# Key tiles of 8 grid rows by 16 columns in a neighbourhood attention, in place of 16 by 8

## The chip, the cores and the metric

The kernel runs on one core of a Trainium2 chip. The metric is the device time of one execution in microseconds. Before the change the median of three runs is 632.16 us (632.13 to 632.43).

## The reference

One layer over 1024 latent tokens on a grid of 16 rows by 64 columns and 256 context tokens, width 1024. A conditioned RMS norm and one input projection give eight groups of 512 columns; half feed an attention of 8 heads of 64, half a gated short convolution; both are gated, joined and projected out. Cut to the attention:

```python
row_start = clip(qi - 4, 0, rows - 8)            # 8 rows of keys for each query row
col_start = clip(cols - 8, 0, 64 - 16)           # 16 columns of keys for each query column
s_lat = (q_rot . k_rot) * scale + rpb[dr, dc]    # -inf outside the window
s_ctx = (q_plain . kc) * scale                   # all 256 context keys
p = softmax(concat(s_lat, s_ctx))
o = p_lat @ v + p_ctx @ vc
```

All of it is in float32, and the kernel keeps that precision by splitting each operand into a high and a low part and multiplying three times (`mm3`, line 68), or twice in the scores, where the two halves of a query lie below each other in the 128 partitions.

## The kernel before

**Order of tokens.** After the norm, the transposed activations are stored block by block: 8 blocks of 128 tokens, a block being 16 grid rows by 8 columns (`rows_of`, line 686; `blocked`, `by_row`, `natural`, lines 378 to 385). Block j is therefore also key tile j. Everything after the projection sees tokens in this order until the output projection puts them back (`put_y`).

**Projection.** 32 tiles (four pairs of heads by eight token blocks) are projected in the loop at the end of the projection stage; `turn_qk` (line 237) transposes queries and keys of two blocks, splits them in high and low and spills them to DRAM. In the same loop `bias_tables` (line 749) spreads the padded bias in DRAM by two rounds of transfers on SyncE's queue (SP), and `masked_tables` (line 928) adds the window mask and stores one table of 128 by 3 by 384 for each head.

**Attention.** The loop at line 1360 calls `quarter(n)` (line 1110) for n = 0 to 35; n is a *tick*, four to a head, called quarters g = n % 4 here. The order of instructions on every engine is fixed by the order in which the code emits them (`strict`, line 1355). In tick n, TensorE does

- the maxima of quarter e = n - 2: `pmx` transposes two blocks of the running maximum `mx`, VectorE reduces them (`rm`), `pmx` spreads them back and ScalarE copies them to `mg`;
- the context products of quarter o = n - 3 (`ctx_out`), in `po`;
- the scores of two key tiles of tick n (`scores`, in `pss`): tile j against the query blocks j-1 to j+1, which is 384 columns, or 256 at the edges. A head's tiles go 0; 1, 2; 3, 4; 5, 6; 7, and tile 7 shares a tick with tile 0 of the next head, so that 33 ticks have scores;
- the context scores of quarter n (`ctx_scores`, in `pc`);
- steps of *filler*: the rest of the projection (`pu`, six matmuls of 512 columns a step); `TICKS[n]` (line 33) says how many;
- between them the value products of tick o (`lat_out`, `pv`, lines 1048 to 1058), three per tile and PSUM bank, added up in two banks of 512 query columns for each head. Tiles 3 and 4 straddle the border of the banks.

In the same tick VectorE adds the bias to the scores, updates `mx` with the context (`ctx_max`) and the two tiles (`lat_max`), subtracts the maximum from those of quarter e, makes the low parts of the exponentials (`plc`, `pll`), and does what the filler needs (`ul`, `cv`). ScalarE takes each exponential twice, once rounded and once whole. At the end of a bank `finish` copies it out and stores it. Loads for the next head are issued from SP during the head before (lines 1360 to 1368).

Of the kernel before, what the change touches and what calls it, by code (L numbers as in the profile page):

```python
# [19 lines left out]
P = 128  # L20
D = 1024
T = 1024
# [10 lines left out]
TICKS = [2, 3, 3, 3, 3, 2, 3, 3, 2] + 2 * (8 * [3] + 2 * [4]) + 3 * [3] + [4, 4, 3, 2]  # L33
# [6 lines left out]
def body(tc, es, x, ctxt, w_ada, b_ada, w_in, q_g, k_g, rpbr, w_out, vecs, cst, out):  # L40
# [196 lines left out]
    def turn_qk(pp, p, two, t0):  # L237
# [140 lines left out]
    def blocked(v):  # L378
        return v.rearrange("p (b r c) -> p b r c", b=4, r=16)

    def by_row(v):
        return v.rearrange("p (r b c) -> p b r c", r=16, b=4)

    def natural(v, half):
        return v.rearrange("p (r b c) -> p b r c", r=16, b=8)[:, 4 * half:4 * half + 4]

    def blocked8(v):
        return v.rearrange("p (b r c) -> p b r c", b=8, r=8)
# [8 lines left out]
    def conv_group(i, done=None):  # L397
# [10 lines left out]
        def multiplied(half, ps):  # L408
            def product():
                to, of = (rows8(cu[:, 1:T + 1], half, 8), blocked8) if done else (natural(cu[:, 1:T + 1], half), blocked)  # L410
# [47 lines left out]
        def gains():  # L458
            for half, ps in sorted(done[CBG].items()) if done else ():
                for q in range(2):  # L460
                    def gain(half=half, ps=ps, q=q):
                        v = rows8(cvs[q][:], half, 4)
                        dve.tensor_tensor(v, blocked8(ps[:])[:, 4 * q:4 * q + 4], v, ALU.mult)
# [205 lines left out]
    def modulated(hi, lo, ps, k, w, on, between=None):  # L669
# [5 lines left out]
        if n == 512:  # L675
            hv = hv.rearrange("p (r b c) -> p r b c", r=8, b=8)
# [9 lines left out]
    def rows_of(v, half):  # L686

        return v.rearrange("p (b r c) -> p r b c", b=8, r=16)[:, 8 * half:8 * half + 8]
# [7 lines left out]
    def turn(half, k, on, between=None):  # L696

        modulated(rows_of(hh[k], half), rows_of(hl[k], half),
                  pts.pop((half, k))[:].rearrange("p (r b c) -> p r b c", r=8, b=8), k, 0, on, between)
# [49 lines left out]
    def bias_tables():  # L749

        for kc in range(8):
            sp.dma_start(t2_d[kc], bass.AP(rpbr.tensor, rpbr.offset + 7 - kc, [[31, NH * 31], [1, 24]]))
        t2 = t2_d[:]
        for kr in range(16):
            if kr % 4 == 0:
                yield
            sp.dma_start(t3_d[:, kr], bass.AP(t2.tensor, t2.offset + (15 - kr) * 24,
                                              [[744, NH], [NH * 744, 8], [1, 384]]))
# [169 lines left out]
    def masked_tables():  # L928
# [3 lines left out]
        view = lambda t, n: t.rearrange("p (o r c) -> p o r c", r=16, c=8)  # L932
        for h in range(NH):
            raw = bmp.tile([P, 512], F32, name="braw", tag="kc_s", bufs=2)
            sp.dma_start(raw[:, :384], t3_d[h].rearrange("a b c -> (a b) c"))
# [4 lines left out]
            stores.append(lambda h=h: sp.dma_start(t4_d[h], bt[:].rearrange("p v n -> p (v n)")))  # L940
# [43 lines left out]

    class head:
# [27 lines left out]
        def masks(self):  # L1013
            self.bt = bmp.tile([P, 3, 384], F32, name="bt", tag="bt", bufs=2)
            sp.dma_start(self.bt[:].rearrange("p v n -> p (v n)"), t4_d[self.h])

        def ctx_scores(self, g):
# [6 lines left out]
            sc = ap.tile([P, 2, 256], F32, name="sc", tag="sc", bufs=3)  # L1024
# [8 lines left out]
        def span(self, j):  # L1033
            return max(j - 1, 0), min(j + 1, NB - 1)

        def scores(self, j, ps):
            lo, hi = self.span(j)
            n = (hi - lo + 1) * P
            q = self.q[:, 0, lo * P:(hi + 1) * P]
            for l in range(2):  # L1040
                pe.matmul(ps[:, :n], self.k[:, j // 2, l, j % 2 * P:(j % 2 + 1) * P], q, start=(l == 0), stop=(l == 1))

        def lat_max(self, j, sb):
            lo, hi = self.span(j)
            m = mx[:, lo * P:(hi + 1) * P]
            dve.tensor_tensor(m, m, sb[:, :(hi - lo + 1) * P], ALU.max)

        def pv(self, bank, cols, j, ph, pl, last):
# [3 lines left out]
            o_ = self.po[bank][0:HD + 1, cols]  # L1052
# [5 lines left out]
        def lat_out(self, j, ph, pl):  # L1058
            lo, hi = max(j - 1, 0), min(j + 1, NB - 1)
            for a, b in ((lo, min(hi, 3)), (max(lo, 4), hi)):  # L1060
                if a <= b:
                    src = slice((a - lo) * P, (b + 1 - lo) * P)
                    self.pv(a // 4, slice((a % 4) * P, (b % 4 + 1) * P), j,
                            ph[:, src], pl[:, src], (a // 4, j) in ((0, 4), (1, 7)))

        def ctx_exp(self, g):
# [3 lines left out]
            ph = ap.tile([P, 2, 256], F32R, name="phc", tag="phc", bufs=2)  # L1070
            pl = ap.tile([P, 2, 256], F32R, name="plc", tag="plc", bufs=2)
# [5 lines left out]
        def ctx_out(self, g):  # L1077
            ph, pl = self.cps.pop(g)
            for i in range(2):
                self.pv(g // 2, slice((g % 2) * 256, (g % 2 + 1) * 256), NB + i, ph[:, i], pl[:, i], False)  # L1080

        def finish(self, bank):

            ob = ap.tile([P, 512], F32, name="ob", tag="ob", bufs=1)
            act.copy(ob[0:HD + 1], self.po[bank][0:HD + 1])
# [3 lines left out]
    def pair_of(n):  # L1089

        h, g = divmod(n, 4)
        two = [(h, 0), (h - 1, 7)] if g == 0 else [(h, 2 * g - 1), (h, 2 * g)]
        return [(i, heads[h_], j) for i, (h_, j) in enumerate(two) if 0 <= h_ < NH]

    def both(v, n, pair):
# [428 lines left out]
```

## Time and profile before

| | |
|---|---|
| median of three runs | 632.16 us |
| the profiled execution, in all | 632.35 us |
| its span in the trace | 630.6 us |
| TensorE busy | 624.0 us |
| VectorE busy | 439.1 us |
| ScalarE busy | 330.0 us |
| granted TensorE clock | 1.00 |
| first scores of the attention | 267.1 us |
| last filler of the attention ends | 539.3 us |

How to read it: PE is the matmuls of TensorE, PEld its weight loads, DVE is VectorE, ACT is ScalarE, POOL is GpSimd, SP is SyncE. Names such as `po<-phl,v` give the tile written and the tiles read, without buffer numbers. Nearly every instruction of these stages passes through one helper and has line 55, so groups are told apart by their tiles. The chain of waits follows the work that ended last back in time; its rows give a start, a length, and a number of instructions. A row of the busy time by stretches gives the stretch, its length, the busy time and the number of instructions of PE, PEld, DVE, ACT and POOL, the granted clock, the share of DMA and its GB/s.

### The profile page before, as it was taken

What the parts mean: (1) busy time and instruction counts of PE and PEld (TensorE: products, weight loads), DVE (VectorE), ACT (ScalarE), POOL (GpSimd) and SP (SyncE); (2) the same over time, 40 slices, a digit from 0 to 9 for tenths busy, and PEclk for the clock granted to TensorE, in tenths of its full rate; (3) what the DMA queues carried; (4) which work ended last, traced back from release to release, by engine and by line L of the source; (5) the groups of instructions that cost most, each with busy time, mean ns of one, the idle gap of its engine ahead of it and who ended that gap; (6) DMA issues with size and microseconds to landing.
All of it is one profiled execution on the core that took longest, in us unless ns stands there. A gap on an engine that the chain in (4) does not pass through costs nothing.

```text
span 630.6 us, 9908 instructions
## 1 busy us (share of the span) xinstructions
PE 624.0 (99%) x3439; PEld 537.1 (85%) x3440; DVE 439.1 (70%) x874; ACT 330.0 (52%) x713; POOL 77.6 (12%) x102
## 2 busy tenths in 40 slices
PE   8999999999999999999999999999999999999998
PEld 3577899999999999888888888888888888888887
DVE  1887859766857755468888889987998865593211
ACT  4676835425625446346676568567775855460000
POOL 1305014123123222000000000000000002002300
PEclk9999999999999999999999999999999999999999
DMA  8983638867775994965383636683842234962731
GB/s 316 358 286 116 180 110 263 258 196 221 267 244 164 295 328 147 324 228 186 129 289 118 217 90 214 191 273 105 271 126 75 60 99 130 374 222 77 268 101 50
DMA packets 103006, 125.60 MB, mean 199 GB/s; under 512 B 9665, under 2 KB 71577, under 8 KB 101676
## 3 DMA queue, kind: packets, MB, share of 16 engines
q1 hardware_dynamic: 96492, 113.38, 54.4%
q10 hardware_dynamic: 6208, 11.05, 5.5%
q0 software_dynamic: 256, 0.54, 0.3%
q8 instruction: 27, 0.44, 0.3%
q14 instruction: 23, 0.19, 0.1%
HBM read 88.09 MB, written 38.62 MB: 201 GB/s over the span
## 4 chain that ended last, share of the span: by engine, by line
PE 98%; DVE 1%; issue 0%; POOL 0%; ACT 0%; POOLq 0%
PE pu L55 30%; PE pacc L55 21%; PE po L55 8%; PE acc L55 6%; PE tr L55 5%; PE pout L75 5%; PE pout L76 5%; PE pout L74 5%; PE cacc L55 4%; PE pss L55 3%; PE pmx L55 2%; PE pc L55 2%; PE trA L55 1%; PE trB L55 1%; POOL xss L55 0%
## 5 line engine op out<-in xcount | busy, mean ns | idle before, releaser
L55 PE MATMUL pu<-h,uh 128*128 128x512 f32 x544 | 169.4, 392 | 0.6 <-DVE cv L55 0.6
L55 PE MATMUL pacc<-w,h 128*128 128x384 f32 x768 | 138.4, 337 | 0.0
L55 PEld LDWEIGHTS pacc<-w,h 128*128 128x128 f32 x768 | 132.7, 188 | 0.2
L55 PEld LDWEIGHTS pu<-h,uh 128*128 128x128 f32 x544 | 98.1, 188 | 18.2 <-DVE cv L55 1.0
L55 PE MATMUL pu<-h,ul 128*128 128x512 f32 x272 | 106.4, 391 | 0.0
L55 PEld LDWEIGHTS pu<-h,ul 128*128 128x128 f32 x272 | 51.1, 188 | 11.3
L55 POOL TENSOR_TENSOR ss<-ss,few 128x4 f32<-128x4 f32 (+1 forms) x40 | 41.9, 1048 | 124.8 <-DVE ss L55 124.8
L75 PE MATMUL pout<-wol,yh 128*128 128x512 f32 (+2 forms) x136 | 51.6, 379 | 0.0
L74 PE MATMUL pout<-woh,yh 128*128 128x512 f32 (+2 forms) x136 | 50.5, 379 | 0.0
L76 PE MATMUL pout<-woh,yl 128*128 128x512 f32 (+2 forms) x136 | 49.8, 379 | 0.0
L55 PE MATMUL acc<-h,w 128*128 128x512 f32 x144 | 38.1, 404 | 0.8 <-ACT h L55 0.8
L55 ACT ACTIVATE sq<-pacc 128x256 f32<-128x256 f32 x32 | 12.3, 386 | 49.1 <-PE pacc L55 47.5
L55 ACT COPY mg<-pmx 128x256 f32<-128x256 f32 x32 | 11.9, 373 | 43.3 <-PE pmx L55 40.8
L55 DVE TENSOR_REDUCE rm<-pmx 128x2 f32<-128x256 f32 x32 | 13.6, 425 | 30.1 <-PE pmx L55 29.8
L55 DVE TENSOR_TENSOR mx<-mx,sb 128x384 f32<-128x384 f32 (+1 forms) x64 | 33.0, 524 | 2.0
L55 DVE TENSOR_REDUCE ss<-sq 128x4 f32<-128x260 f32 (+1 forms) x40 | 15.7, 392 | 23.9 <-ACT sq L55 23.9
L55 ACT ACTIVATE qn<-pacc,ss 128x64 f32<-128x64 f32 x128 | 30.1, 331 | 3.0 <-issue 2.5
L55 PE MATMUL po<-phl,v 128*65 128x256 f32 (+2 forms) x160 | 31.2, 291 | 0.0
L55 PEld LDWEIGHTS acc<-h,w 128*128 128x128 f32 x144 | 25.5, 188 | 6.5 <-ACT h L55 1.2
L55 ACT COPY sc<-pc 128x512 f32<-128x512 f32 x32 | 18.8, 589 | 22.7 <-PE pc L55 22.6
L55 DVE TENSOR_TENSOR pll<-sb,phl 128x768 fp32r<-128x768 f32 (+2 forms) x33 | 28.4, 861 | 1.9 <-ACT sb L55 1.9
L74 PEld LDWEIGHTS pout<-woh,yh 128*128 128x128 f32 x136 | 25.6, 188 | 4.7
(159 smaller groups left out, 1176.7 us busy)
## 6 DMA issues: line engine op xcount, KB each, us to landing
uraw<-in_w_in SPq DMA_DIRECT2D x34, 256.0 KB
q_d<-qs SPq DMA_DIRECT2D x32, 256.0 KB
k_s<-k_d SPq DMA_DIRECT2D x8, 1024.0 KB
q_s<-q_d SPq DMA_DIRECT2D x16, 512.0 KB
wr<-in_w_in SPq DMA_DIRECT2D x40, 192.0 KB
slab<-in_w_ada SPq DMA_DIRECT2D x6, 1024.0 KB
v_d<-vs SPq DMA_DIRECT2D x20, 260.0 KB
v<-v_d SPq DMA_DIRECT2D x16, 325.0 KB
```

Of the source, the lines that this page charges most:

```text
L55: i = emit(*a, **kw)
L74: i = pe.matmul(ps, ah, bh, start=first, stop=False)
L75: pe.matmul(ps, ah, bl, start=False, stop=False)
L76: pe.matmul(ps, al, bh, start=False, stop=last)
```

## The change

A block of 128 tokens becomes 8 grid rows by 16 columns: tile j holds columns 16 (j // 2) onward and the upper or lower eight rows. Tokens in the blocked activations follow as 4 column blocks by 16 rows by 16 columns. Queries are stored column by column, 16 rows to a column: `turn_qk` reorders them while it splits them. A key tile of the upper rows is seen by query rows 0 to 11 only, one of the lower rows by rows 4 to 15, and by the columns from 7 before its own to 8 after; so a tile is multiplied with 12 of every 16 values of a run of 24, 31, 31 or 23 columns.

With it:

- A tick takes the two tiles of one column block, 32 ticks have scores, and the loop has 35 ticks; the last four numbers of `TICKS` become three with the same sum.
- Value products write 12 of every 16 columns of a bank; the column ranges 9 to 40 and 25 to 56 straddle the border at column 32.
- The bias and mask tables become 2 by 47 by 12 in place of 3 by 384; the bias sum takes two instructions in the first and last quarter of a head, one in the others.
- Blocks of the maximum now end half a quarter later: tick n turns blocks 2e + 1 and 2e + 2, so that tick 1 turns block 0 of the first head, and tick 33 the last block.
- Context scores and maxima run one tick ahead (tick 0 does quarters 0 and 1); their copies get four buffers in place of three, the context exponentials one in place of two.
- `finish` reorders a bank while it copies it. Rotary tables and the padded bias are laid out to match on the host.

```diff
-TICKS = [2, 3, 3, 3, 3, 2, 3, 3, 2] + 2 * (8 * [3] + 2 * [4]) + 3 * [3] + [4, 4, 3, 2]
+TICKS = [2, 3, 3, 3, 3, 2, 3, 3, 2] + 2 * (8 * [3] + 2 * [4]) + 3 * [3] + [4, 5, 4]
...
-    t2_d = dr.tile([8, NH * 31, 24], F32, name="t2_d")
-    t3_d = dr.tile([NH, 16, 8, 384], F32, name="t3_d")
-    t4_d = many("t4_d", NH, [P, 3 * 384])
+    t2_d = dr.tile([8, NH * 47, 16], F32, name="t2_d")
+    t3_d = dr.tile([NH, 8, 16, 512], F32, name="t3_d")
+    t4_d = many("t4_d", NH, [P, 1128])
...
-            halves(qs[:, 0], qs[:, 1], pA[:].rearrange("p k i d -> p k (i d)"))
+            halves(*(qs[:, l].rearrange("p k (c r) -> p k c r", r=16) for l in range(2)),
+                   pA[:].rearrange("p k i d -> p k (i d)").rearrange("p k (r c) -> p k c r", r=16))
...
-        h_, l_ = (v.rearrange("p (b r c) -> p b (r c)", b=8, r=16)[:, :, 64 * half:64 * half + 64]
+        h_, l_ = (v.rearrange("p (b r c) -> p b (r c)", b=4, r=16)[:, :, 128 * half:128 * half + 128]
...
-            for n in range(3):
-                dve.tensor_tensor(view(bt[:, n], n), raw[:, :384].rearrange("p (r o c) -> p o r c", r=16, c=8),
-                                  view(mk[:, n], n), ALU.add)
+            by_col = raw[:].rearrange("p (c r) -> p c r", r=16)
+            for a in range(2):
+                rows = slice(4 - 4 * a, 16 - 4 * a)
+                for to, of in ((slice(0, 31), slice(0, 31)), (slice(31, 47), slice(7, 23))):
+                    dve.tensor_tensor(flat(bt)[:, a, to], by_col[:, of, rows], mk[:, a, to], ALU.add)
...
+    def span(j):
+
+        return max(j // 2 * 16 - 7, 0), min(j // 2 * 16 + 24, GW)
+
+    def seen(v, j, cols=None):
+
+        lo, hi = cols or span(j)
+        return v.rearrange("p (c r) -> p c r", r=16)[:, lo:hi, 4 * (j % 2):4 * (j % 2) + 12]
+
+    def cells(v, j, cols=None):
+
+        at = span(j)
+        lo, hi = cols or at
+        return v[:, (lo - at[0]) * 12:(hi - at[0]) * 12].rearrange("p (c r) -> p c r", r=12)
...
         def scores(self, j, ps):
-            lo, hi = self.span(j)
-            n = (hi - lo + 1) * P
-            q = self.q[:, 0, lo * P:(hi + 1) * P]
+            q = seen(self.q[:, 0], j)
             for l in range(2):
-                pe.matmul(ps[:, :n], self.k[:, j // 2, l, j % 2 * P:(j % 2 + 1) * P], q, start=(l == 0), stop=(l == 1))
+                pe.matmul(cells(ps, j), self.k[:, j // 2, l, j % 2 * P:(j % 2 + 1) * P], q, start=(l == 0), stop=(l == 1))
...
-            for a, b in ((lo, min(hi, 3)), (max(lo, 4), hi)):
-                if a <= b:
-                    src = slice((a - lo) * P, (b + 1 - lo) * P)
-                    self.pv(a // 4, slice((a % 4) * P, (b % 4 + 1) * P), j,
-                            ph[:, src], pl[:, src], (a // 4, j) in ((0, 4), (1, 7)))
+            lo, hi = span(j)
+            for bank in range(2):
+                at = max(lo, 32 * bank), min(hi, 32 * bank + 32)
+                if at[0] < at[1]:
+                    self.pv(bank, lambda o: seen(o, j, (at[0] - 32 * bank, at[1] - 32 * bank)), j,
+                            cells(ph, j, at), cells(pl, j, at), (bank, j) in ((0, 5), (1, 7)))
...
+    def turned(n):
+
+        g = n % 4
+        return [b for b, there in (((2 * g + 2) % NB, n + 1 < 4 * NH), (2 * g + 1, n >= 0)) if there][::-1 if g < 3 else 1]
...
-        if live(e):
-            hd, g = heads[e // 4], e % 4
+        blocks = turned(e) if -1 <= e < 4 * NH else []
+        nb = len(blocks)
+        if blocks:
             pm = psm.tile([P, 512], F32, name="pmx", tag="C", bufs=2)
-            for i in range(2):
-                pe.transpose(pm[:, i * P:(i + 1) * P], mx[:, (2 * g + i) * P:(2 * g + i + 1) * P], ident)
+            for i, b in enumerate(blocks):
+                pe.transpose(pm[:, i * P:(i + 1) * P], mx[:, b * P:(b + 1) * P], ident)
...
-        if live(n):
-            heads[n // 4].ctx_scores(n % 4)
+        ctx_now = [m for m in ([0, 1] if n == 0 else [n + 1]) if live(m)]
+        for m in ctx_now:
+            heads[m // 4].ctx_scores(m % 4)
...
+            for at, slot, w_ in (((0, 31, 8), (8, 15, 16)), ((0, 0, 31),), ((0, 0, 31),), ((0, 0, 15), (15, 39, 8)))[n % 4]:
+                dve.tensor_tensor(sb[:, :, at * 12:(at + w_) * 12], sbank[:, :, at * 12:(at + w_) * 12],
+                                  bt[:, :, slot * 12:(slot + w_) * 12], ALU.add)
+            for m in ctx_now:
+                heads[m // 4].ctx_max(m % 4)
...
-        for n in range(4 * NH + 4):
+        for n in range(len(TICKS)):
```

More of the change, by code (lines that the diff above doesn't have):

```diff
@@ L698, in turn @@
         modulated(rows_of(hh[k], half), rows_of(hl[k], half),
-                  pts.pop((half, k))[:].rearrange("p (r b c) -> p r b c", r=8, b=8), k, 0, on, between)
+                  pts.pop((half, k))[:].rearrange("p (r b c) -> p r b c", r=8, b=4), k, 0, on, between)
     def transposed_ctx(k2):
@@ L1131, in quarter @@
             gating.pop(0)
-        if live(e):
-            for i in range(2):
+        if blocks:
+            for i in range(nb):
                 pe.transpose(pm[:, 256 + i * P:256 + (i + 1) * P], rm[:, i:i + 1].broadcast_to([P, P]), ident)
-            act.copy(mg[:, g * 256:(g + 1) * 256], pm[:, 256:512])
+            v, step = mg[:, blocks[0] * P:], (blocks[-1] - blocks[0]) * P or P
+            act.copy(bass.AP(v.tensor, v.offset, [list(v.ap)[0], [step, nb], [1, P]]),
+                     pm[:, 256:256 + nb * P].rearrange("p (i k) -> p i k", i=nb))
         now = pair_of(n)
```

137 lines of the change are left out of this document (58 added, 79 removed).

## The prediction

> **What bounds the kernel now.** I read the page first (busy shares and the chain), then busy time by stretches, then the chain tick by tick, then the timelines of single engines.
>
> ```profile
> PE 624.0 (99%) x3439; PEld 537.1 (85%) x3440; DVE 439.1 (70%) x874; ACT 330.0 (52%) x713; POOL 77.6 (12%) x102
> ...
> PE 98%; DVE 1%; issue 0%; POOL 0%; ACT 0%; POOLq 0%
> ```
>
> TensorE carries 98% of the chain, so an edit counts by what it takes from or adds to TensorE's stream; the other engines count only where TensorE comes to wait for them. In the attention the next engine is close: a row of the busy time by stretches shows VectorE busy 53.49 of 60 us and ScalarE 38.81, at full clock.
>
> ```profile
> 360.00:420.00 60.00, 59.83 (x348) 51.12 (x347) 53.49 (x91) 38.81 (x65) 0.13 (x2) 1.00 0.57 183
> ```
>
> TensorE's pace in a tick comes from the chain of waits (start, length, count). A matmul's own duration contains its latency; the chain's length divided by its count is the spacing, and that is what counts here.
>
> ```profile
> 408.65 0.71 PE po L55 x6
> 409.36 0.24 PE pmx L55 x2
> 409.60 0.48 PE pss L55 x4
> 410.08 0.48 PE pc L55 x4
> 410.56 1.39 PE pu L55 x6
> 411.95 1.04 PE po L55 x6
> ...
> 416.90 0.71 PE pss L55 x4
> ...
> 419.49 1.07 PE po L55 x12
> ```
>
> The first row is six context products of 256 columns: 0.118 us each. 411.95 is six value products of 384: 0.173 us. 419.49 mixes six of 256 with six of 128: (1.07 - 0.71)/6 = 0.060 us for 128. Scores: four of 256 take 0.48, four of 384 take 0.71, so 0.23/(4 x 128) = 0.449 ns a column. Value products: (0.173 - 0.118)/128 = 0.43 ns a column.
>
> **Scores.** A head's eight key tiles now cover 6 x 384 + 2 x 256 = 2816 query columns; afterwards 12 rows times 24, 31, 31 and 23 grid columns, for two key tiles each: 2 x (288 + 372 + 372 + 276) = 2616. Each is multiplied twice (two halves of the key), eight heads: 200 x 2 x 8 x 0.449 ns = **-1.44 us**. The counts of before, by form:
>
> ```profile
> L55 PE MATMUL pss<-q_s,k_s 128*128 128x384 f32 x96 | 22.7, 358 | 0.0
> ...
> L55 PE MATMUL pss<-q_s,k_s 128*128 128x256 f32 x32 | 6.0, 304 | 0.0
> ```
>
> The moving side is then read in runs of 12 of every 16 values. No row has such runs. The nearest is the early projection, which reads eight runs of 64 a matmul: nine take 2.06 us, 0.229 each, against 1.39/6 = 0.231 for the flat ones of the tick above. So a run costs nothing visible there, and I take nothing; upper bound, the skipped columns cost as if read (16 of 16): 384, 496, 496, 368 columns, 3488 against 2816, +672 x 2 x 8 x 0.449 = +4.83 us instead of -1.44.
>
> ```profile
> 41.77 2.06 PE acc L55 x9
> ```
>
> **Value products.** Three per tile and PSUM bank. Before, per head: four of 384, four of 256, two of 128: 3 x (4 x 0.173 + 4 x 0.118 + 2 x 0.060) = 3.85 us. After: four of 288 (0.118 + 32 x 0.43 ns = 0.132), four of 276 (0.127), and, because columns 9 to 40 and 25 to 56 straddle the bank's border at column 32, two of 96 and two of 84. These are short, and each loads its own weights. What a load costs is seen where a 128-column weight meets only 128 moving columns, at the end of the output projection:
>
> ```profile
> 625.03 0.27 PE L75 MATMUL pout<-wol,yh 128*128 128x128 f32 x1
> 625.14 0.27 PE L76 MATMUL pout<-woh,yl 128*128 128x128 f32 x1
> ```
>
> 0.11 us apart, though 128 columns stream in 0.060 above: there the load sets the pace. Scaled to the 65 weight columns of a value product it is 0.11 x 65/128 = 0.056 us, an estimate from that row. So 96 and 84 columns cost 0.058, not the 0.047 and 0.042 that their columns would give: 3 x (4 x 0.132 + 4 x 0.127 + 4 x 0.058) = 3.80 us. Eight heads: **-0.4 us** with the loads as floor; lower bound, with streaming alone, 3.64, so -1.7 us.
>
> The result is written to 12 of every 16 PSUM columns. No row of before writes PSUM in runs; the flat rows are the nearest, and I take no surcharge. Upper bound, as for the reads: columns paid by 16, 384, 368, 128 and 112 wide, 3 x (4 x 0.173 + 4 x 0.166 + 4 x 0.060) = 4.79 us a head, +0.94 x 8 = +7.5 us instead of -0.4. [...]
>
> **The start of attention.** The maxima are now turned two blocks at a time in ticks 2 to 33; afterwards the same 64 blocks take ticks 1 to 33, and tick 1 turns block 0. That puts a wait where there was none: the turn needs tick 0's two maxima, which need both context copies that tick 0 now makes (quarters 0 and 1). The present tick 0, from the timeline:
>
> ```profile
> 268.80 0.64 PE L55 MATMUL pc<-q_s,kc_s 128*128 128x256 f32 x4
> ...
> 269.47 0.59 ACT L55 COPY sc<-pc 128x512 f32<-128x512 f32 x1 [1.35 <-PE pc L55]
> ...
> 270.09 0.43 DVE L55 TENSOR_TENSOR mx<-pc,sc 128x256 f32<-128x256 f32 x1 [0.86 <-ACT sc L55]
> 270.55 0.43 DVE L55 TENSOR_TENSOR mx<-mx,sb 128x256 f32<-128x256 f32 x1
> ```
>
> Four scores of 288 instead of two of 256 start pc 0.30 later, at 269.10. TensorE then has eight pc (0.96) and six pu (1.39) and is at the turn at 271.45. ScalarE copies the first pc at 269.77 and the second from 270.36 to 270.95; VectorE's second context maximum starts 0.62 after the copy began, 270.98, and ends at 271.41; two maxima of 288 at 0.46 end at 272.33. TensorE waits **0.9 us**, with the scores of tick 1 and all later work behind it in its queue. Then the turned block must be reduced and broadcast with no context product between. This is how tick 2 looks now:
>
> ```profile
> 276.09 0.23 PE pmx L55 x2
> 276.33 0.02 issue
> 276.35 0.44 DVE rm L55
> 276.79 0.04 issue
> 276.83 0.43 PE pmx L55 x2
> ```
>
> TensorE stands 0.5 us; with one block instead of two the reduction is some 0.13 shorter: **0.4 us** more, tick 2 keeping its own. Together +1.3 us. Bounds: 0.8 if half the wait on the maxima is hidden, 2.0 if VectorE is behind.
>
> **VectorE, ScalarE, and where a stall goes.** Four passes a tick shrink with the columns (sum with the bias, subtraction of the maximum, remainder, running maximum).
>
> ```profile
> L55 DVE TENSOR_TENSOR mx<-mx,sb 128x384 f32<-128x384 f32 x48 | 26.8, 558 | 1.7
> L55 DVE TENSOR_TENSOR sb<-pss,bt 128x768 f32<-128x768 f32 x24 | 22.8, 951 | 0.6 <-PE pss L55 0.6
> ...
> L55 DVE TENSOR_TENSOR mx<-mx,sb 128x256 f32<-128x256 f32 x16 | 6.2, 422 | 0.3
> ```
>
> (558 - 422)/128 = 1.06 ns a value and 0.15 us an instruction: three passes of 200 values and the bias sum with one instruction more (two in quarters 0 and 3) save 4 x 200 x 1.06 - 150 = 0.7 us of VectorE a head, 5.6 us in all. Hardly any of it is on the chain. Where TensorE does wait for VectorE it is inside a tick, as here at a projection's buffer:
>
> ```profile
> 402.60 0.69 DVE cv L55
> 403.29 0.04 issue
> 403.33 1.65 PE pu L55 x6
> ```
>
> That is tick 19, a fourth quarter: pu takes 1.65 instead of 1.39 and starts 0.15 late, 0.4 us in all. Its scores shrink to four of 276 (0.52 instead of 0.71), so TensorE arrives 0.19 earlier, and the remainder ahead of cv grows from 512 values to 576 (0.07): 0.25 us worse. Two more ticks stand for the rest of these waits:
>
> ```profile
> 469.12 0.40 PE pmx L55 x2
> 469.51 0.24 PE po L55 x2
> 469.75 0.04 issue
> ...
> 478.18 0.23 PE pmx L55 x2
> ...
> 480.99 1.65 PE pu L55 x6
> ```
>
> Tick 28's turn takes 0.40 instead of 0.23: it waits for the maxima that tick 27, a fourth quarter, ends with, and VectorE's lighter pass there (552 values for 768) should remove the 0.2. Tick 29's pu starts 2.81 after its turn where turn, po, pmx, pss and pc need 2.37, and takes 0.26 longer, 0.7 us; it is a second quarter, whose scores and remainder shrink by 0.02 each: unchanged. Net of the three 0; together they are worth 1.3 us.
>
> **What I cost at nothing.** The bias tables are made during the projection, four sums of 372 and 192 values instead of three of 384: 4 x 0.15 + 1128 x 1.06 ns = 1.80 against 1.67 us a head. TensorE hides it there, busy 60.00 of 60 us beside a VectorE at 38.84; without that cover it costs 8 x 0.13 = 1.0 us. The table's transfers on SP's queue:
>
> ```profile
> 180.00:240.00 60.00, 60.00 (x359) 58.51 (x358) 38.84 (x110) 28.80 (x109) 16.79 (x19) 1.00 0.77 254
> ...
> 68.95 5.44 SPq L55 DMA_DIRECT2D t_d<-in_rpb  x8
> ...
> 89.59 2.66 SPq L55 DMA_DIRECT2D t_d<-t_d  x4
> ```
>
> 376 runs instead of 248 each would make the first 2.8 us longer at worst; 15 us lie between it and the next that needs it. The second kind carries 512 instead of 384 values a run, a third more bytes. Context scores run a tick earlier, so q and kc of the next head are needed a tick earlier; but the last scores of the head before the last end a tick earlier too, which is when those buffers come free. One buffer for the context weights instead of two: the context product that frees it ends at 409.36, early in the tick, ahead of the exponentials that refill it. The tail: the tick list sums to 110 steps of filler before and after; one tick less with the same filler moves nothing. Transposed reads of PSUM in the query split and the final copy lie on ScalarE at 52%.
>
> **Sum.** Profiled execution: 630.6 us span, 632.35 us in all (1.75 around it), 0.19 over the median 632.16. 632.35 - 1.44 - 0.4 + 1.3 = 631.8, by the median **631.6 us**.
>
> **Rivals.**
> - *Faster, 629.7:* the short products stream (-1.3 more) and half of the 1.3 us of waits for VectorE goes with its 5.6 us (-0.6). For: VectorE was at 89%. Against: the load row, and waits that are tick latency, not throughput.
> - *Slower, 639.5: runs in PSUM.* Value products pay for the skipped columns: +7.9. It decides from 6 ns a product (288 of them carry the 1.8 us from 631.6 to 633.4). For: no row excludes it. Against: the runs of 64 on the read side cost nothing. [...]
> - *Nothing saved by the 12 rows, 637.9:* the scores' reads pay for 16, +6.3; the change then doesn't shorten the stream as it says.
> - *Slower, 633.6:* the fourth quarters' shorter scores uncover VectorE in all eight heads, 8 x 0.25. Against: only one of them shows a wait now.
>
> **Chances and range.** Forecast 0.46, faster rival 0.30, PSUM runs 0.10, read runs 0.04, fourth quarters 0.10. 0.2% of 632.16 is 1.26 us, about what can be told from no change: faster 0.30 (below 630.9), same 0.46, slower 0.24 (above 633.4). The range, 629.0 to 635.5, reaches past the faster rival and the fourth quarters and leaves out the two run surcharges.
>
> **What would show it.** Scores of 372 spaced 0.170 and of 276 0.127 (runs cost nothing) or over 0.2; short products at 0.058; value products of 288 at 0.132 or well over; in tick 1 a wait of pmx for the maxima near 0.9 and for rm near 0.4; 33 rather than 32 turns. I am wrong if that wait is absent, or if cv waits appear in most fourth quarters.

## The result, and the profile after

The changed kernel takes 633.20 us (median of 18 runs, 631.76 to 635.71) where the kernel before takes 632.14 (18 runs, 631.11 to 632.52): a ratio of 1.0023 by the means of the runs, 95% interval 1.0013 to 1.0034 (1.0017 by the medians). The forecast was 631.6. Two things are seen at once: the change is slower by 1.06 us in the median instead of faster by 0.5, and its runs lie over 4.0 us where those of before lie over 1.4.

The profiled execution took 633.06 us with a span of 631.3, at a granted clock of 1.00. The page's busy shares and the chain that ended last:

```profile
PE 622.9 (99%) x3488; PEld 538.6 (85%) x3488; DVE 433.5 (69%) x889; ACT 326.7 (52%) x712; POOL 78.6 (12%) x102
...
PE 89%; DMA 4%; DVE 3%; issue 1%; ACT 1%; POOL 0%; SPq 0%; ACTq 0%; DVEq 0%; POOLq 0%
```

TensorE and VectorE are busy for less time than before, 1.1 and 5.6 us, so the saving is there; but TensorE no longer carries 98% of the chain. What TensorE waited for from the attention on, in the view of its waits (us in total, times, longest), of after and then of before; the rows of `acc` and `tr`, which lie ahead of the attention, are left out:

```profile
...
PE pu L55 <- DVE cv L55: 0.9, 2, 0.5
PE pmx L55 <- DVE rm L55: 0.9, 2, 0.5
PE pmx L55 <- DVE mx L55: 0.8, 1, 0.8
...
PE pout L74 <- ACT yh L1436: 0.3, 1, 0.3
```

```profile
...
PE pu L55 <- DVE cv L55: 0.6, 2, 0.4
PE pmx L55 <- DVE rm L55: 0.5, 1, 0.5
```

The waits for `mx` and the second `rm` are the forecast's wait in tick 1. The wait of `pout` for `yh` is new and was in no part of the prediction: it lies in the output projection, after the attention. The stretches put it in place (start and end, length, PE, PEld, DVE, ACT and POOL busy, granted clock, DMA share, GB/s); first after, then before, with the borders at the last value product and the first and last output product:

```profile
267.00:282.00 15.00, 13.26 (x72) 11.04 (x71) 9.11 (x18) 5.50 (x12) 0.00 (x0) 1.00 0.77 255
282.00:521.50 239.50, 238.46 (x1438) 206.77 (x1437) 198.55 (x353) 154.33 (x260) 0.27 (x4) 1.00 0.49 161
521.50:539.30 17.80, 17.80 (x81) 14.74 (x80) 10.53 (x17) 9.92 (x15) 3.40 (x6) 1.00 0.63 187
539.30:628.20 88.90, 88.59 (x408) 74.18 (x407) 34.72 (x55) 15.72 (x27) 10.25 (x8) 1.00 0.51 177
```

```profile
267.00:282.00 15.00, 14.48 (x77) 12.31 (x75) 9.68 (x18) 6.87 (x14) 0.00 (x0) 1.00 0.79 264
282.00:524.10 242.10, 241.45 (x1398) 206.34 (x1397) 206.19 (x348) 158.37 (x261) 0.26 (x4) 1.00 0.49 160
524.10:539.20 15.10, 15.10 (x70) 12.52 (x69) 7.80 (x13) 7.55 (x12) 3.39 (x6) 1.00 0.61 183
539.20:627.50 88.30, 88.30 (x409) 74.27 (x407) 35.03 (x55) 16.12 (x28) 10.23 (x8) 1.00 0.53 184
```

Read the last row of each: the same 408 products take 88.9 us instead of 88.3, and in after TensorE is idle in between. Read the first: TensorE is idle 1.74 us of the first 15 instead of 0.52. The last value product comes 2.6 us earlier (521.5 for 524.1), but that time is only filled with filler; the attention as a whole ends where it ended.

Spacing of TensorE's start times from the first scores to the first output product, added up by the tile written (my sums over the trace, us; an interval belongs to the instruction that opens it, so a wait stands with the instruction ahead of it):

```
tile              before   after
pss (scores)       23.35   21.90   -1.46
po  (products)     56.41   55.61   -0.80   (phl, pll -0.50; context -0.30)
pu  (filler)      165.46  167.29   +1.82
pmx (maxima)       10.52   10.89   +0.36
pc  (ctx scores)   16.35   16.64   +0.30
all               272.10  272.32   +0.23
```

The columns saved are there; the waits, and pauses of TensorE without a wait, which stand in pu, pmx and pc, take back a little more.

**Runs of 12 cost nothing.** In after's chain of waits (start, length, count), in the first head:

```profile
286.14 0.51 PE pss L55 x4
...
288.51 0.79 PE po L55 x6
289.29 2.75 PE pu L55 x12
...
295.57 1.09 PE po L55 x12
296.67 2.84 PE pu L55 x12
```

The four scores are of 276 columns, 0.128 us each, forecast 0.127; four of 372, at 300.68, take 0.68, 0.170 each, as forecast. Six value products of 288 columns take 0.132 us each, as forecast for flat ones; the row at 295.57 is six of 276 at 0.127 and six of 96, which leaves (1.09 - 0.76)/6 = 0.055 us for a short one, forecast 0.058. Both rivals about runs, in PSUM and in the reads, fall with these rows.

**Behind the short products.** The two rows of twelve filler products are not alike: behind the products of 288 columns they take 2.75 us, behind those that end with three of 96 columns 2.84. In the trace the second product of the latter row starts 0.305 us after the first, where 0.227 is usual, and no wait for a semaphore is shown. The same stands at eight places of after, one in each head, wherever three products of 96 columns come directly ahead of filler: 0.298 to 0.305 us each time, 0.60 us in all (my sums over the trace). Before has no such place, because its products of 128 columns never stand ahead of filler. What makes the pauses is shown by no run. So the value products, 0.50 us shorter among themselves, are 0.1 us dearer with what stands behind them.

**The output stage.** Where TensorE stands still there (timeline of after: start, length, engine, line, what, idle before):

```profile
567.62 0.39 PE L76 MATMUL pout<-woh,yl 128*128 128x512 f32 x1
568.32 0.50 PE L74 MATMUL pout<-woh,yh 128*128 128x512 f32 x1 [0.31 <-ACT yh L1436]
568.66 0.39 PE L75 MATMUL pout<-wol,yh 128*128 128x512 f32 x1
```

The matmul at 568.32 is the first that uses the block of y for f = 3, the seventh in `FORDER`. Its second half is cast by ScalarE here, first in after and then in before:

```profile
566.61 0.62 ACT L1436 CAST yh<-tb 128x512 fp32r<-128x512 f32 x1 [0.96 <-DMA tb<-y_d]
...
567.66 0.61 ACT L1436 CAST yh<-tb 128x512 fp32r<-128x512 f32 x1
```

```profile
565.89 0.62 ACT L1425 CAST yh<-tb 128x512 fp32r<-128x512 f32 x1 [1.24 <-DMA tb<-y_d]
...
566.94 0.62 ACT L1425 CAST yh<-tb 128x512 fp32r<-128x512 f32 x1
```

In before it is there at 567.56 and first used at 570.92, after 140 other output products: 3.4 us in hand. In after it is there at 568.27, 0.7 later, and wanted after 126 products, at 539.29 + 126 x 0.227 = 567.9. The order of this stage isn't written out (`strict` is emptied at the end of the attention); the scheduler that makes it put 14 products fewer ahead. Why it did is not shown by any run here. With nothing in hand, whatever makes y late in one execution shows in the time (the runs lie over 4.0 us; over 1.0 in a_tail8b, below, with 144 products ahead).

### The profile page after: what moved, and what is told of

It reads as the page before. It is cut to its first block, busy times and chain, and to the rows that moved or that the text cites. A ratio compares the mean times of both kernels' runs of the same rounds, so it can differ in the third digit from the quotient of the medians.

```text
span 631.3 us, 10013 instructions
## 1 busy us (share of the span) xinstructions
PE 622.9 (99%) x3488; PEld 538.6 (85%) x3488; DVE 433.5 (69%) x889; ACT 326.7 (52%) x712; POOL 78.6 (12%) x102
## 4 chain that ended last, share of the span: by engine, by line
PE 89%; DMA 4%; DVE 3%; issue 1%; ACT 1%; POOL 0%; SPq 0%; ACTq 0%; DVEq 0%; POOLq 0%
PE pu L55 27%; PE pacc L55 21%; PE po L55 8%; PE acc L55 6%; PE tr L55 5%; PE cacc L55 4%; PE pout L74 3%; PE pout L76 3%; PE pout L75 3%; PE pss L55 3%; PE pmx L55 2%; PE pc L55 2%; DMA tb<-y_d 2%; DMA woraw<-in_w_out 2%; PE trA L55 1%
## 5 line engine op out<-in xcount | busy, mean ns | idle before, releaser
L55 DVE TENSOR_REDUCE rm<-pmx 128x2 f32<-128x256 f32 (+1 forms) x33 | 13.7, 416 | 33.8 <-PE pmx L55 33.7
L55 ACT COPY mg<-pmx 128x256 f32<-128x256 f32 (+1 forms) x33 | 12.1, 366 | 47.1 <-PE pmx L55 37.7
L55 DVE TENSOR_TENSOR mx<-mx,sb 128x372 f32<-128x372 f32 (+2 forms) x64 | 31.8, 498 | 2.0
L55 PE MATMUL po<-phl,v 128*65 128x276 f32 (+2 forms) x192 | 32.0, 269 | 0.0
L1462 DVE TENSOR_TENSOR ot<-pout,xr 128x512 f32<-128x512 f32 (+2 forms) x9 | 5.7, 632 | 36.5 <-PE pout L76 36.5
L76 PEld LDWEIGHTS pout<-woh,yl 128*128 128x128 f32 x136 | 25.6, 188 | 4.7
```

Of the source, the lines that this page charges most:

```text
L55: i = emit(*a, **kw)
L76: pe.matmul(ps, al, bh, start=False, stop=last)
L1462: dve.tensor_tensor(ot[:, c], ps[c.start][:, c], xr[:, c], ALU.add)
```

## The experiments

Names beginning with a are edits of the kernel after, those with b of the kernel before. Medians in us with the range of the runs; the ratio, by the means, is to the kernel before, run on the same chip at the same time, with its 95% interval. The runs were made in groups on different chips, and the median of the kernel before lay between 631.96 and 632.51 in these groups. Medians of different groups can therefore be compared only to about half a microsecond.

| run | median (range) | ratio | attention | output |
|---|---|---|---|---|
| before | 632.14 (631.11 to 632.52) | | 272.10 | 88.30 |
| after | 633.20 (631.76 to 635.71) | 1.0023 (1.0013 to 1.0034) | 272.32 | 88.91 |
| a_tail8 | 641.20 (639.93 to 641.52) | 1.0138 (1.0124 to 1.0152) | 272.48 | 96.08 |
| b_tail8 | 640.21 (639.49 to 642.56) | 1.0132 (1.0115 to 1.0149) | 272.11 | 95.93 |
| a_start | 632.78 (631.34 to 634.38) | 1.0009 (1.0001 to 1.0018) | 271.96 | 90.46 |
| a_both | 640.43 (639.50 to 641.46) | 1.0133 (1.0117 to 1.0148) | 271.93 | 96.44 |
| a_tail8b | 632.44 (631.87 to 632.85) | 1.0003 (0.9994 to 1.0012) | 272.32 | 88.30 |
| b_tail8b | 632.09 (631.48 to 632.71) | 0.9996 (0.9987 to 1.0005) | 272.11 | 88.30 |
| a_start2 | 630.36 (630.05 to 631.50) | 0.9970 (0.9959 to 0.9981) | 270.70 | 88.34 |
| a_both2 | 630.33 (629.93 to 631.33) | 0.9972 (0.9960 to 0.9983) | 270.60 | 88.30 |
| b_cover126 | 634.96 (633.39 to 635.66) | 1.0037 (1.0023 to 1.0050) | 271.93 | 90.46 |
| b_cover108 | 640.52 (640.38 to 642.14) | 1.0137 (1.0121 to 1.0153) | 271.99 | 97.30 |
| a_cover108 | 641.29 (640.60 to 641.92) | 1.0140 (1.0127 to 1.0154) | 272.34 | 97.43 |
| b_both2 | 636.34 (635.88 to 637.32) | 1.0065 (1.0052 to 1.0078) | 276.74 | 88.30 |
| a_first | 639.35 (638.58 to 641.47) | 1.0122 (1.0104 to 1.0139) | 278.33 | 88.30 |
| b_mid | 636.58 (634.62 to 636.70) | 1.0065 (1.0051 to 1.0079) | 276.54 | 88.30 |
| a_first2 | 631.78 (631.22 to 632.45) | 0.9995 (0.9986 to 1.0005) | 271.82 | 88.30 |
| b_mid2 | 632.25 (631.71 to 632.94) | 1.0000 (0.9991 to 1.0009) | 272.18 | 88.30 |
| a_firstmid | 631.40 (630.48 to 632.32) | 0.9985 (0.9976 to 0.9994) | 271.25 | 88.30 |

The last two columns are from the profiled execution of each: from the first scores to the first output product, and from there to the last output product.

### Theory 1: the output stage's cover

**a_tail8 and b_tail8.** The first eight output tiles, not six, are multiplied key tile by key tile, and TensorE keeps that order:

```diff
-    first = {t: bank("pout", "SCO"[t // 2]) for t in range(6)}
+    strict[:] = [pe]
+    first = {t: bank("pout", "SCOU"[t // 2]) for t in range(NB)}
...
-    for n, (nh, t) in enumerate([(0, 6), (0, 7)] + [(1, t) for t in range(NB)]):
+    for n, (nh, t) in enumerate([(1, t) for t in range(NB)]):
```

> The changed kernel, with the output stage alone put another way: the products of the first eight output tiles (six column tiles of the first half before, eight here) run key tile by key tile in a fixed order on TensorE, so 144 instead of 126 matmuls (144 x 0.227 = 32.7 us instead of 28.6) lie ahead of the first product that needs the block of y that came late (567.66 us in the profile of after). Theory 1, the loss is a wait of TensorE for y in the output stage that differs from run to run: the profiled run has no gap over 0.1 us between output products (0.56 in after), the runs lie as close as those of before (within 1.5 us, after 4.0), the median falls by 1.0 to about 632.2. Theory 2, the loss is made ahead of the output stage (the wait for maxima in tick 1 and VectorE): the median stays at 633.2 less the 0.56 of the one profile, 632.6 at the least, and the spread of 4 us stays. Theory 3, runs of 12 elements slow TensorE: 633.2.

> The kernel before, with the same other order of the output stage. Theory 1: before has 140 matmuls ahead of the late block of y and no gap there in its profile, so nothing is to be had: 632.1, within 0.3. If the order itself is cheaper (fewer changes of tile, weight loads better hidden) before gains what after gains, about 1 us: 631.1.

Both became 8 us slower, mostly by one new wait and not by y (TensorE's waits in a_tail8):

```profile
PE pout L55 <- DVE ot L1465: 6.0, 1, 6.0
```

The ninth tile asked for a bank that VectorE emptied only seventh. No gap lies ahead of it, so y had been in time; but the total says nothing on the theory.

**a_tail8b and b_tail8b.** The same edit, with the banks given out in the order in which they come free:

```diff
-        ps = {c.start: bank("pout", "USC"[(n + i) % 2 + i]) for i, c in enumerate(pieces)}
+        ps = {c.start: bank("pout", "SCOU"[(n // 2 + i) % 4]) for i, c in enumerate(pieces)}
```

> The eight-tile order on the changed kernel again, with the PSUM banks given out in the order in which they come free: the first tile of the second half now takes the bank that was emptied first (at 578.6 us in the run before, 3.7 us ahead of its use), where it had taken the one emptied seventh, with a wait of 6.0 us for VectorE. Theory 1 (the loss is TensorE's wait for y in the output stage): no gap over 0.1 us from the first output product to the last, which is 88.3 us as in before (88.9 in after), runs within 1.5 us of each other, median 632.2. Theory 2 (lost ahead of the output stage): 632.6 to 633.2 with 4 us of spread.

> The same order and banks on the kernel before. Theory 1: nothing to gain, 632.2 within 0.3. If the order itself is cheaper, about 1 us less: 631.2.

After fell by 0.76 us, to the level of the kernel before in the same group of runs (632.38; the ratio's interval contains 1), and its runs drew together from 4.0 to 1.0 us; before did not move beyond the noise (0.05 us under its first median, 0.29 under that of its group). One of the 24 runs of the kernel before in that group stands out at 634.27; the other 23 lie over 1.5 us. The stretch of a_tail8b's output stage, idle nowhere:

```profile
538.70:627.00 88.30, 88.30 (x409) 74.27 (x407) 35.41 (x56) 15.87 (x28) 10.24 (x8) 1.00 0.52 179
```

So most of the loss, 0.76 of the 1.06 us by the medians, and the wide spread came from the output stage.

**b_cover126, b_cover108 and a_cover108.** The counter-test: take the cover away from the kernel before, and more of it from both. The output products stand in a fixed order with the first six tiles through the first six f, then (126) the seventh tile or (108) nothing, then f = 3 and 7:

```diff
+    strict[:] = [pe]
     first = {t: bank("pout", "SCO"[t // 2]) for t in range(6)}
-    for f in FORDER:
+    for f in FORDER[:6]:
         for t in first:
             out_mm(first[t], 0, t, f)
+    first[6] = bank("pout", "U")
+    for f in FORDER[:6]:
+        out_mm(first[6], 0, 6, f)
+    for f in FORDER[6:]:
+        for t in first:
+            out_mm(first[t], 0, t, f)
...
```

> The kernel before, with its output products in a fixed order that puts 126 matmuls ahead of the first product with the block of y that is made seventh (f = 3), as after has them, where before's own order has 140. In before's profile that block's second cast ends at 567.55 us; 126 matmuls end at 539.18 + 126 x 0.227 = 567.8, so the cover is gone but for 0.2 us. Theory 1: the margin of 3.4 us, not a slower y, is what after lost: the kernel before gets after's spread (runs up to 634 or more) and a median 0.3 to 1.0 higher, 632.5 to 633.1. If after's loss is its later y (0.7 us later) alone, or not in this place at all: 632.2, spread as before's.

> The same with no product ahead of that block but those of the first six tiles: 108 matmuls, used up at 563.7. Theory 1: TensorE waits there for y until 567.6 or a little later in the profile, 3.9 us, and the median is 632.2 + 3.9 = 636.1. If y is made earlier where it is wanted earlier, or other work takes the place: under 634.

> The same on the changed kernel: 108 matmuls used up at 563.8, y there at 568.3: 4.5 us of wait, 632.4 (its time with 144 ahead) + 4.5 = 636.9. With after itself (126 ahead, 633.2) and the run with 144 ahead (632.4) this gives the time against the cover: theory 1 has about 0.23 us a matmul below 127 and nothing above.

With 126 ahead the kernel before is 2.4 us slower than with its own order, and its runs spread over 2.3 us. That is more than expected, and not by the wait that was expected: in the profiled execution the high part, `yh`, was cast at 566.60, in time for the product at 566.85, and the loss is a wait for `yl`, as the fixed order asks for the low part two products after the high one (timeline of b_cover126):

```profile
566.85 0.39 PE L55 MATMUL pout<-woh,yh 128*128 128x512 f32 x1
567.08 0.40 PE L55 MATMUL pout<-wol,yh 128*128 128x512 f32 x1
569.10 0.50 PE L55 MATMUL pout<-woh,yl 128*128 128x512 f32 x1 [1.62 <-DVE yl L1426]
```

So this run shows that the kernel before has nothing to spare with 126 products ahead, but not after's wait for `yh` itself. With 108 the waits are in the place and about the size expected: for `yh` 3.9 us in b_cover108 and 4.7 in a_cover108, against 3.9 and 4.5. The totals are 4.4 us worse than the expectations. Part is the same wait for `yl` (1.2 and 1.4), and part the clock, as a_cover108's stretches show:

```profile
568.20:570.00 1.80, 0.56 (x2) 0.00 (x1) 1.80 (x4) 0.80 (x2) 0.00 (x0) 0.55 0.14 52
570.10:575.20 5.10, 5.06 (x12) 4.00 (x13) 1.19 (x2) 0.00 (x0) 0.00 (x0) 0.50 0.00 0
575.30:600.00 24.70, 24.70 (x110) 20.44 (x109) 6.20 (x9) 0.00 (x0) 10.21 (x8) 1.00 0.55 191
```

After the wait the granted clock is 0.50 for 5 us: twelve products at 0.43 us instead of 0.227. In the profiles nothing is lost in the output stage with 140 to 144 products ahead; with 126 ahead after loses 0.6 us and a_start, below, 2.2, both by waits for `yh` (a_start by two, one of them 54 products earlier), and b_cover126 loses 2.2 by the wait for `yl`; with 108 it is 9 us. Theory 1 stands, and where cover was taken away by a fixed order the price was more than a microsecond for each microsecond, because the low part and the clock came on top.

### Theory 2: the start of the attention

**a_start and a_both.** Three filler steps moved within ticks 1 and 2 (one ahead of tick 1's maxima transposes, one of each tick between the two sets); a_both has a_tail8's edit besides.

```diff
+        if n == 1:
+            next(fill)
+            ticks -= 1
         if blocks:
             pm = psm.tile([P, 512], F32, name="pmx", tag="C", bufs=2)
...
+        if n in (1, 2):
+            next(fill)
+            ticks -= 1
         do_dves(3)
```

> The changed kernel, with three filler steps moved within ticks 1 and 2: one of tick 1 ahead of the transposes of the maxima, one of tick 1 and one of tick 2 between these and the transposes that spread the row maxima. Theory 2 (the start is part of the loss): the wait for VectorE's maxima (0.8 us in after) and both waits for the reduced maxima (0.9) go, attention from the first scores to the first output product takes 270.6 instead of 272.3, the median falls by 1.7 to 631.5, with the 4 us of spread left. If TensorE only waits later for the same VectorE work, 0 to 0.3 us are gained: 633.0.

> Both of these edits on the changed kernel. Theories 1 and 2 together: 633.2 - 1.0 - 1.7 = 630.5, runs within 1.5 us of each other, 0.3% faster than before. Theory 1 alone: 632.2. Theory 2 alone: 631.5 with the wide spread. If an earlier end of attention only makes the output stage wait longer for y (y is made by the other engines, not by TensorE), 631.9 or more.

A miss: the attention gained 0.36 us, not 1.7. In a_start's waits the one in tick 1 is gone, but another stands in tick 2, where the steps were taken from:

```profile
PE pout L74 <- ACT yh L1442: 1.3, 2, 1.1
PE pmx L55 <- DVE mx L55: 1.0, 1, 1.0
...
PE pmx L55 <- ACT sb L55: 0.4, 1, 0.4
```

The first row is theory 1 again: same order with 126 ahead, and an output stage of 90.46 us in this execution, 2.2 more than without a wait. a_both carries a_tail8's wait for a bank and says nothing by its total.

**a_start2 and a_both2.** One step more in each of ticks 0, 1 and 2, so that all later steps come up to three places earlier and the pure filler at the end becomes shorter; a_both2 has a_tail8b's edit besides:

```diff
-TICKS = [2, 3, 3, 3, 3, 2, 3, 3, 2] + 2 * (8 * [3] + 2 * [4]) + 3 * [3] + [4, 5, 4]
+TICKS = [3, 4, 4, 3, 3, 2, 3, 3, 2] + 2 * (8 * [3] + 2 * [4]) + 3 * [3] + [4, 5, 4]
...
+        if n in (1, 2):
+            next(fill)
+            ticks -= 1
         do_dves(3)
```

> The changed kernel with one filler step more in each of ticks 0, 1 and 2, taken from the 17.6 us of pure filler behind the last value product; in ticks 1 and 2 it stands between the two sets of maxima transposes. Theory 2: tick 1's wait for maxima (0.8) and the two for reduced maxima (0.9) go and do not come back in tick 2, since no later tick loses a step: attention 270.5 instead of 272.3, and the median 1.8 lower, 631.4, with the wide spread of after. If the earlier filler is only replaced by a longer wait for y in the output stage (the last products of attention end 2 us later, and y with them): 632.8 or more.

> Both on the changed kernel. Theories 1 and 2: 632.2 - 1.8 = 630.4, runs within 1.5 us of each other, 0.3% below before. Theory 1 alone: 632.2; theory 2 alone: 631.4 with the wide spread.

a_start2 is 0.3% faster than before, 1.0 us under its expectation, and its attention is 1.6 us shorter than after's. The stretch at the start has no idle time left:

```profile
267.60:282.00 14.40, 14.40 (x78) 12.21 (x77) 7.67 (x16) 4.49 (x10) 0.00 (x0) 1.00 0.74 245
```

That its runs lie close (1.5 us) goes against its expectation, and agrees with theory 1: the scheduler put 142 products ahead of f = 3 in this kernel, and its output stage takes 88.34 us. So it needed no second edit, and a_both2 is no faster.

**b_both2, a_first and b_mid.** To see whether the start's wait is the change's own: before with both edits; after with one step more in tick 0 alone; before with one step more in tick 2, between its maxima transposes, from a tick in the middle. All three have the eight-tile order with a_tail8b's banks.

```diff
 b_both2
-TICKS = [2, 3, 3, 3, 3, 2, 3, 3, 2] + 2 * (8 * [3] + 2 * [4]) + 3 * [3] + [4, 4, 3, 2]
+TICKS = [3, 4, 4, 3, 3, 2, 3, 3, 2] + 2 * (8 * [3] + 2 * [4]) + 3 * [3] + [4, 4, 3, 2]
 a_first
+TICKS = [3, 3, 3, 3, 3, 2, 3, 3, 2] + 2 * (8 * [3] + 2 * [4]) + 3 * [3] + [4, 5, 4]
 b_mid
+TICKS = [2, 3, 4, 3, 3, 2, 3, 3, 2] + 8 * [3] + [4, 3] + 8 * [3] + 2 * [4] + 3 * [3] + [4, 4, 3, 2]
```

> The kernel before with both edits of a_both2 (the eight-tile order, one filler step more in each of ticks 0 to 2). Theory 2, the added wait for maxima is the change's own: before has only the 0.5 us for reduced maxima to lose, 632.1 - 0.5 = 631.6, and a_both2 (630.3) stands 1.3 under it, near the 1.84 that the prediction had for fewer columns on TensorE. If the start's edit is worth as much in any kernel of this build: 630.4, and the change itself is worth nothing.

> The changed kernel with the eight-tile order (632.4 by itself) and one filler step more in tick 0 alone, from the tail. If the wait for maxima in tick 1 is lost cover of one step (0.8 us by the profile of after), it goes and nothing comes in its place: attention 271.4 instead of 272.3, 631.5. If VectorE is what limits the start, it comes back in tick 2 as it did where steps were only moved: 632.2.

> The kernel before with the eight-tile order and with one filler step between the two sets of maxima transposes of tick 2, its only wait at the start (0.5 us), the step taken from a tick in the middle and not from the tail, where taking three cost 2.7 us. 632.1 - 0.5 = 631.6; 1.3 above a_both2 (630.3), which is then what the change gives where both kernels are put right. If the step is missed in the tick that gives it: 632.1 or more.

All three lost 4 to 7 us, none at the start. In a_first the wait for `mx` went and did not come back in tick 2, but (its waits):

```profile
PE pu L55 <- ACT zs L55: 5.6, 2, 2.9
...
PE pmx L55 <- ACT ob L55: 1.1, 1, 1.1
PE pmx L55 <- DVE rm L55: 0.9, 2, 0.5
```

The timeline of ScalarE shows what the filler waits for when it goes on to the next unit, the bank that `zs` empties:

```profile
383.18 0.81 ACT L55 ACTIVATE phl<-sb 128x744 fp32r<-128x744 f32 x1
384.02 0.82 ACT L55 ACTIVATE sb<-sb 128x744 f32<-128x744 f32 x1
384.87 1.28 ACT L55 ACT_TABLE_LOAD   x1
386.16 1.08 ACT L55 ACTIVATE zs<-pu 128x512 f32<-128x512 f32 x2
```

The unit's activation stands behind the tick's exponentials (0.81 and 0.82 us) and a table load (1.28 us). With every step one place earlier, two changes of unit fall where ScalarE hasn't got there; b_mid and b_both2 each meet one such wait (2.8 and 2.6 us). How many steps a tick takes is thus tied to where the units end, and these runs tell nothing on the start but a_first's one point.

**a_first2, b_mid2 and a_firstmid.** The steps are given back by tick 7, so that the rest meets what it met; all have the eight-tile order, b_mid2 and a_firstmid the steps between the transposes in tick 2 and in ticks 1 and 2.

```diff
 a_first2
+TICKS = [3, 3, 3, 3, 3, 2, 3, 2, 2] + 2 * (8 * [3] + 2 * [4]) + 3 * [3] + [4, 5, 4]
 b_mid2
+TICKS = [2, 3, 4, 3, 3, 2, 3, 2, 2] + 2 * (8 * [3] + 2 * [4]) + 3 * [3] + [4, 4, 3, 2]
 a_firstmid
+TICKS = [3, 4, 4, 2, 2, 2, 3, 2, 2] + 2 * (8 * [3] + 2 * [4]) + 3 * [3] + [4, 5, 4]
```

> The changed kernel with the eight-tile order and one filler step more in tick 0, given back in tick 7, so that from tick 8 on every tick meets the steps that it meets in after; in a_first, where every later step came one tick place early, two changes of filler unit met a ScalarE that was not done (5.6 us). If the wait for maxima is only lost cover: attention 271.4 instead of 272.3, 632.4 - 0.9 = 631.5. If tick 7 misses its step: 632.2 or more.

> The kernel before with the eight-tile order and one filler step more in tick 2, between its two sets of maxima transposes, given back in tick 7. Its one wait at the start (0.5) goes and no later tick meets other steps: 632.1 - 0.5 = 631.6. If tick 7 misses its step: 632.1 or more.

> The changed kernel with the eight-tile order and the three steps of a_both2 in ticks 0 to 2, given back in ticks 3, 4 and 7. If the 1.8 us of a_both2 are those of the start's waits alone: 632.4 - 1.8 = 630.6. If part of them came from the later steps falling better (its waits for VectorE's cv, 0.9 us in after, are gone in it): 631.0 to 631.6. The difference to b_mid2 is what the change gives with both starts put right: 1.0 by the first, 0 to 0.6 by the second.

Against the same kernel without the edit, a_tail8b, which ran in another group: a_first2 gains 0.66 us by the medians (632.44 to 631.78) and 0.50 in the profile's attention, where the wait for `mx` is gone and 0.3 us of waiting for `rm` has come up at the turn of tick 8, right behind the tick that gave its step; a_firstmid gains 1.04 and 1.07. b_mid2 gains nothing, since the wait for `rm` (0.5) that left tick 2 came back at the turn of tick 8. In before, then, the start had nothing to give that way; in after it had. What is left to a_both2 (1.1 us by the medians, 0.65 by the profiles' attention) agrees with the second case of the expectation, that the later steps fall better. a_firstmid still has the waits for `cv` (0.9) and two for `rm` (0.6), now in ticks 4 and 8, behind ticks that gave a step; the list of a_both2 has neither, and has 1.3 us for ScalarE's `ob` and 0.4 for `zs`.

The kernel before was not brought to a better plan of steps in three attempts, so what the change is worth with both at their best stays open. With the same output order and the plans as they were it costs 0.35 us (632.44 against 632.09, in one group; just clear of the noise, and 0.21 in the profiles' attention). With the start changed in both, a_firstmid stands 0.85 us under b_mid2 in one group, but b_mid2's plan had not helped the kernel before.

## Why the prediction was wrong

The sum stood at 631.6; measured 633.20. In the profiles the forecast was -0.54 us and the difference came out at +0.71: attention +0.23 instead of -0.54, the output stage +0.61 instead of nothing, and the first scores 0.12 earlier. So two steps failed, one in each stage. That the time still lies in the stated range is luck: neither the mechanism forecast nor that of a rival put it there.

- **Scores, -1.44:** right, -1.46.
- **Value products, -0.4:** the step that failed in the attention, a mis-sized term. Among themselves they came out as forecast, -0.50. The short ones took 0.055 us with 96 columns and 0.049 with 84 (for the latter the mean spacing of the 48 in after's trace), where the prediction works out 0.056 for both and puts 0.058 into the sum, which is 0.2 us of the term. That the loads of weights set that pace was the author's estimate, and no run shows it. But it counted the spacing of the short products alone, and not what stands behind them: eight pauses in the filler, 0.60 us. Together +0.1.
- **Runs of 12, nothing:** right on both sides: 0.132 us for 288 columns written so, 0.170 for 372 read so.
- **The start, +1.3:** right, by the waits 0.84 + 0.38 us. That the first is a lack of cover, which one filler step in tick 0 takes away, was not part of the forecast; a_first2 shows it, with 0.3 us coming back elsewhere.
- **"Net of the three 0" for the waits on VectorE:** right for the three that it names. The wait for `cv` in tick 19 grew by 0.28 (forecast 0.25), that of tick 29 by 0.02 (forecast nothing), and the turn of tick 28 became 0.18 shorter (forecast 0.2). Context products among which before had short waits gave 0.30 more; against that the turns of ticks 27 and 32, which stand in no term, became 0.38 longer. A few other pauses of TensorE in the filler, in before too, are not explained by any run.
- **"One tick less with the same filler moves nothing":** this is the step that failed in the output stage. It looked at the count of filler steps alone. The output stage behind it was taken as given, but it is ordered by a scheduler, and it came out with 126 products ahead of the seventh block of y instead of 140, which cost 0.61 us in the profile and 0.76 in the median. The margin of 3.4 us that before's trace held could have been read there: when a cast ends and when its product starts. That the scheduler would spend it could not be read there, and why it did stays open. No rival named this place; the slower rival that came nearest in time (633.6) had another mechanism, and the `cv` waits did not spread to all fourth quarters.

## What to carry to other kernels

Ahead of a change, look at how much each later stage has in hand, not only at where TensorE waits now: before's output stage showed no wait and was 3.4 us from one, and the scheduler, left free, spent 3.2 of them (14 products of 0.227). A wider spread of the runs at full clock (4.0 us instead of 1.4) was the sign here that such a margin was gone. Where short matmuls are counted, look also at the spacing of what follows them (here up to 0.305 us instead of 0.227). And where filler steps are dealt out by hand, moving one step moves every later change of unit against the other engines (in a_first two such changes waited 5.6 us for ScalarE): give the step back nearby if only one place is to be tested.

## What the runs showed of the hardware

After some waits of TensorE of less than 3 us the granted clock was about half. After 2.58 us of idle time in b_both2 and 2.94 in a_first the next stretch ran at 0.50 to 0.53; after 2.68 us in a_first, 80 us earlier, it stayed at 1.00 (stretches that begin shortly ahead of the first matmul after the wait: b_both2, then two of a_first):

```profile
530.50:533.00 2.50, 2.32 (x6) 1.84 (x7) 0.00 (x0) 1.17 (x3) 0.42 (x1) 0.50 0.90 281
```

```profile
386.50:390.00 3.50, 3.19 (x20) 2.81 (x21) 1.27 (x3) 2.10 (x5) 0.00 (x0) 1.00 0.00 0
467.60:470.40 2.80, 2.66 (x6) 2.03 (x7) 0.00 (x0) 0.58 (x2) 0.00 (x0) 0.53 0.09 16
```

So in these runs the length of the wait alone did not decide: 2.58 us was followed by 0.50 and 2.68 by 1.00. What else decides is not shown. The price behind the waits was about 2.4 us in a_cover108 (twelve products at 0.43 instead of 0.227).
